# GpSimd makes every third low part of the weights in the first block of a two-block network

## The chip, the cores and the metric

One NeuronCore of a Trainium2 chip runs the kernel. The metric is the device time of one execution in microseconds, the median of several runs; less is better. The engines are named as in the profile: PE (TensorE), ACT (ScalarE), DVE (VectorE), POOL (GpSimd), SP (SyncE, which here issues DMAs).

## What is computed

Two networks follow each other on 256 tokens of width 1024, all in fp32. The first block has two layers; each multiplies the normed tokens by `w_in`, runs three kinds of attention over the parts, and multiplies the result by `w_out`:

```
def hybrid_layer(x, norm_w, w_in, ..., w_out):
    h = rmsnorm(x, norm_w)
    proj = jnp.matmul(h, w_in).astype(jnp.float32)
    (aq, ak, av, ag, bq, bk, bv, bg, cq, ck, cv, co, cg, ci, cf) = jnp.split(proj, cuts, axis=-1)
    ya = moba_attention(aq, ak, av) * silu(ag)          # 8 heads, softmax with a slope per head
    yb = head_norm(retention(rotate(bq), rotate(bk), bv), ret_norm_w) * silu(bg)
    yc = head_norm(mlstm(silu(conv(cq)), silu(conv(ck)), cv, ci, cf) * sigmoid(co), ...) * silu(cg)
    return x + jnp.matmul(concat([ya, yb, yc]), w_out)
```

The second block (two layers of gated feed-forward, attention and convolution, steered by modulation vectors `c @ w_ada`) takes the rest of the time; the change does not touch it.

## The kernel before

Tokens lie transposed in SBUF, 128 channels on the partitions. Every fp32 product is made of three matmuls in a faster format: each operand is split in a high part, rounded to that format, and a low part, the remainder; high x high, high x low and low x high are summed in PSUM (lines 412 to 414, and 443 to 445 where the weights are the moving operand).

The weights stream in from HBM, once, in the order of their use. They are cut into 628 numbered pieces of up to 1024 columns on 128 partitions. `Weights.load` (line 278) has SP load a chunk into one of five buffers `wraw`. `Weights.ahead` splits a piece into two tiles of a pool with four buffers: ACT copies it into `whi` (line 296), DVE subtracts `whi` from it into `wlo` (line 297). `get` calls `ahead` for two pieces beyond the one that is wanted, so the splits of piece i are put into the program ahead of the matmuls of piece i - 2. Each engine works through its instructions in the order of the program; waits on semaphores hold them back. The pieces called ada (16 of the first 104) are not split: DVE multiplies and sums them directly (line 558).

The first block uses pieces 0 to 103: 0 to 52 in layer 0, 53 to 103 in layer 1. `dense` and `dense_tok` run the products; after each step of the contraction they call `side.hook`, which puts a small step of the attention work into the program (generators `mlstm`, `retention`, `moba_items`, `heads_b`, `heads_c`). So DVE's queue holds, in one order: splits, ada pieces, evacuation of products (rotation at lines 838 to 845, of which `bkp` is one result), and attention steps (`put` of scores at line 826, row maxima at line 877, head norms at lines 704 to 718, and line 855).

GpSimd has little to do in the first block: after three memsets it issues the DMAs of 24 decay and slope tables, one for each head (`table`, line 638, three buffers; for the first four also a copy of one column at line 637 that orders the DMA). A table is asked for in the program where its use stands, and its DMA waits for the reader of the table three before it (line 826 or 877, on DVE). Elsewhere, in the second block's attention, GpSimd runs casts and subtractions of 128 columns (lines 1232 to 1234).

Of the kernel before, what the change touches and what calls it, by code (L numbers as in the profile page):

```python
# [9 lines left out]
F32 = mybir.dt.float32  # L10
F32R = mybir.dt.float32r
AF = mybir.ActivationFunctionType
OP = mybir.AluOpType
# [142 lines left out]
def piece_floats(s):  # L156
    return len(s[3]) * sum(n for _, n in s[4])
# [73 lines left out]
def tile_hybrid_then_dit(ctx: ExitStack, tc: tile.TileContext, wst, xT, ctxT, c_d, cols_d, base_d, first_d, heads_d,  # L231
                         mix_d, rpb_d, out, dbg=None):
    nc = tc.nc
    PE, ACT, DVE, POOL, SP = nc.tensor, nc.scalar, nc.vector, nc.gpsimd, nc.sync
# [22 lines left out]
    class Weights:  # L257
# [24 lines left out]
        def ahead(self, upto):  # L282
            while self.split < min(upto, len(self.pieces)):
                i = self.split
                c, at, s = self.pieces[i]
                while self.loaded <= c:
                    self.load()
                f = piece_floats(s)
                r = self.raw[c]
                if s[0] in "at":  # L290
                    self.parts[i] = r
                else:
                    pool, nm = (self.late, "late") if (self.keys[i][0][0], self.keys[i][1][:3]) in LATE else (wsp, "w")
                    hi = pool.tile([128, PIECE], F32R, name=nm + "hi")
                    lo = pool.tile([128, PIECE], F32R, name=nm + "lo")
                    ACT.activation(hi[:, :f], r[:, at:at + f], AF.Copy)  # L296
                    DVE.tensor_tensor(lo[:, :f], r[:, at:at + f], hi[:, :f].bitcast(F32), op=OP.subtract)  # L297
                    k = len(s[3])
                    self.parts[i] = tuple(x[:, :f].rearrange("p (k c) -> p k c", k=k) for x in (hi, lo))
                self.split += 1  # L300
                if i + 1 == len(self.pieces) or self.pieces[i + 1][0] != c:
                    while self.loaded < min(c + RAW_BUFS, len(chunks)):
                        self.load()
# [1271 lines left out]
```

## Time and profile before

| | |
|---|---|
| median of 3 runs | 2225.05 us (2223.63 to 2230.49) |
| the profiled execution | 2223.87 us, span 2222.1 us |
| busy share of the span | PE 99%, DVE 72%, ACT 42%, POOL 6% |
| granted TensorE clock, mean | 0.998 |
| line 297 on DVE, `wlo` | 460 instructions, 539.5 us |
| first block | about 0 to 325 us of the span |

All times below are of the profiled execution, in us from the start of the span. A row of the timeline gives the start, the duration, the engine, the line, the operation and what it writes and reads with its size; in brackets stands how long the engine was idle before it, and what ended that. Matmuls are pipelined, so PE counts as busy also where it runs below its pace. An instruction that is held inside the engine, for a port for instance, has a longer duration; it does not show as idle time.

### The profile page before, as it was taken

The page shows a single profiled execution, that of the slowest core. Times are in us where ns is not written, and L with a number is a line of the kernel's source. Part 1 is how long each engine was busy: PE and PEld are TensorE (multiplying, and loading weights), DVE is VectorE, ACT ScalarE, POOL GpSimd, SP SyncE. Part 2 cuts the span into 40 slices and gives each one's busy share as a digit, 9 for nine tenths or more (in the row PEclk, how much of TensorE's full clock was granted, in tenths as well). Part 3 has the DMA queues.
Part 4 walks back from the last instruction along what each step waited for, and adds up shares of the span by engine and source line. Part 5 has one row for each costly group of instructions (what it writes and reads, how often), then busy time and mean ns, then how long its engine had stood idle before and what let it go on. Part 6 is the DMA issues. An engine that isn't in the chain of part 4 may idle for free.

```text
span 2222.1 us, 33972 instructions
## 1 busy us (share of the span) xinstructions
PE 2192.7 (99%) x13010; PEld 1915.7 (86%) x13010; DVE 1610.6 (72%) x2922; ACT 943.1 (42%) x1546; POOL 131.0 (6%) x283
## 2 busy tenths in 40 slices
PE   8999999999999999999999999999999999999998
PEld 7898898888889877788988888988888898899998
DVE  7998989758848966547773766776577588767555
ACT  7465464212333366524432223332222344755444
POOL 1000000000000144100000000000000012300000
PEclk9999999999999999999999999999999999999999
DMA  8565557546642221234353556254456433255563
GB/s 271 180 203 182 184 173 228 174 137 214 205 140 72 95 72 51 68 102 161 103 177 116 183 180 188 87 180 154 134 187 191 140 110 114 65 182 179 190 198 114
DMA packets 99282, 337.99 MB, mean 152 GB/s; under 512 B 11312, under 2 KB 15664, under 8 KB 99120
## 3 DMA queue, kind: packets, MB, share of 16 engines
q1 hardware_dynamic: 95600, 326.39, 45.5%
q0 software_dynamic: 2976, 8.92, 1.3%
q8 instruction: 102, 1.67, 0.3%
q14 instruction: 60, 0.49, 0.1%
q10 hardware_dynamic: 544, 0.52, 0.1%
HBM read 334.74 MB, written 1.05 MB: 151 GB/s over the span
## 4 chain that ended last, share of the span: by engine, by line
PE 84%; issue 7%; DVE 6%; ACT 1%; DMA 1%; POOL 0%; DVEq 0%; SPq 0%; ACTq 0%; POOLq 0%
PE psd L413 22%; PE psd L412 22%; PE psd L414 22%; PE psd L396 3%; PE psd L397 3%; PE psd L395 3%; PE pso L1282 2%; DVE wlo L297 2%; PE pst L1270 1%; PE psd L443 1%; PE psd L444 1%; PE psd L445 1%; PE pss L1236 1%; DMA table<-in_heads_dram 1%; PE pss L1237 1%
## 5 line engine op out<-in xcount | busy, mean ns | idle before, releaser
L412 PE MATMUL psd<-hh,whi 128*128 128x512 f32 (+1 forms) x2240 | 770.2, 344 | 0.3 <-DVE XT L1031 0.2
L413 PE MATMUL psd<-hl,whi 128*128 128x512 f32 (+1 forms) x2240 | 768.3, 343 | 0.0
L414 PE MATMUL psd<-hh,wlo 128*128 128x512 f32 (+1 forms) x2240 | 766.7, 343 | 0.6 <-DVE wlo L297 0.5
L297 DVE TENSOR_TENSOR wlo<-wraw,whi 128x1024 fp32r<-128x1024 f32 (+2 forms) x460 | 539.5, 1176 | 231.8 <-ACT whi L296 228.1
L296 ACT ACTIVATE whi<-wraw 128x1024 fp32r<-128x1024 f32 (+2 forms) x460 | 468.1, 1020 | 553.1 <-PE psd L413 375.8
L414 PEld LDWEIGHTS psd<-hh,wlo 128*128 128x128 f32 x2240 | 420.3, 188 | 52.9 <-DVE wlo L297 1.0
L412 PEld LDWEIGHTS psd<-hh,whi 128*128 128x128 f32 x2240 | 420.5, 188 | 52.3 <-issue 1.2
L413 PEld LDWEIGHTS psd<-hl,whi 128*128 128x128 f32 x2240 | 420.7, 188 | 51.6 <-issue 1.0
L558 DVE CUSTOM_DVE_ANT_0 prod<-wraw,rows,cols 128x1024 f32<-128x1024 f32 x256 | 328.5, 1283 | 122.1 <-DMA wraw<-in_wst_dram 115.8
L412 PE MATMUL psd<-ah,whi 128*128 128x512 f32 (+1 forms) x576 | 207.8, 361 | 0.0
L413 PE MATMUL psd<-al,whi 128*128 128x512 f32 (+1 forms) x576 | 207.8, 361 | 0.0
L414 PE MATMUL psd<-ah,wlo 128*128 128x512 f32 (+1 forms) x576 | 207.8, 361 | 0.0
L1107 ACT ACTIVATE silu<-psd 128x512 f32<-128x512 f32 (+1 forms) x88 | 47.9, 544 | 228.1 <-PE psd L414 221.6
L413 PEld LDWEIGHTS psd<-al,whi 128*128 128x128 f32 x576 | 108.1, 188 | 16.9
L414 PEld LDWEIGHTS psd<-ah,wlo 128*128 128x128 f32 x576 | 108.1, 188 | 16.9
L412 PEld LDWEIGHTS psd<-ah,whi 128*128 128x128 f32 x576 | 108.1, 188 | 16.7
L585 DVE SCALAR_TENSOR_TENSOR XT<-psd,mods,XT 128x256 f32<-128x256 f32 x216 | 93.3, 478 | 39.9 <-PE psd L414 25.4
L371 ACT ACTIVATE ah<-silu 128x512 fp32r<-128x512 f32 (+1 forms) x88 | 50.4, 574 | 158.3 <-DVE silu L1108 157.9
L443 PE MATMUL psd<-whi,hh 128*128 128x512 f32 (+1 forms) x224 | 88.1, 394 | 10.4 <-ACT whi L296 7.7
L1108 DVE TENSOR_TENSOR silu<-psd,silu 128x512 f32<-128x512 f32 (+1 forms) x88 | 54.7, 622 | 57.3 <-ACT silu L1107 57.3
L444 PE MATMUL psd<-whi,hl 128*128 128x512 f32 (+1 forms) x224 | 87.0, 388 | 0.0
L445 PE MATMUL psd<-wlo,hh 128*128 128x512 f32 (+1 forms) x224 | 85.4, 386 | 0.0
(341 smaller groups left out, 2985.2 us busy)
## 6 DMA issues: line engine op xcount, KB each, us to landing
wraw<-in_wst_dram SPq DMA_DIRECT2D x564, 512.0 KB, 4.0
wraw<-in_wst_dram SPq DMA_DIRECT2D x48, 384.0 KB, 3.1
table<-in_heads_dram POOLq DMA_DIRECT2D x24, 192.0 KB, 3.3
rows<-in_cvec_dram SPq DMA_DIRECT2D x6, 512.0 KB, 5.7
rpb<-in_rpb_dram POOLq DMA_DIRECT2D x24, 128.0 KB, 2.4
wraw<-in_wst_dram SPq DMA_DIRECT2D x8, 264.0 KB, 4.2
wraw<-in_wst_dram SPq DMA_DIRECT2D x8, 256.0 KB, 2.7
XT<-in_xT_dram SPq DMA_DIRECT2D x4, 256.0 KB, 5.3
```

The lines of the kernel that those rows point to most:

```text
L296: ACT.activation(hi[:, :f], r[:, at:at + f], AF.Copy)
L297: DVE.tensor_tensor(lo[:, :f], r[:, at:at + f], hi[:, :f].bitcast(F32), op=OP.subtract)
L395: PE.matmul(p[:, n0:n1], hi, rh[:, k, n0:n1], start=k == 0, stop=False)
L396: PE.matmul(p[:, n0:n1], hi, rl[:, k, n0:n1], start=False, stop=False)
L412: PE.matmul(o, hi[:, kk, c], rh[kr][:, n0:n1], start=first and k == 0, stop=False)
L413: PE.matmul(o, hi[:, kk, c], rl[kr][:, n0:n1], start=False, stop=False)
L414: PE.matmul(o, lo[:, kk, c], rh[kr][:, n0:n1], start=False, stop=last and k == total - 1)
L443: PE.matmul(p, lh[:, k, c], hi[:, kk], start=k == 0, stop=False)
L444: PE.matmul(p, ll[:, k, c], hi[:, kk], start=False, stop=False)
L445: PE.matmul(p, lh[:, k, c], lo[:, kk], start=False, stop=k == 7)
L558: DVE.tensor_tensor_reduce(v(prod()), v(r), rows[s], 1.0, col("b_ada_2", b), op0=OP.mult, op1=OP.add, accum_out=mods.rearrange("p l c s -> ...
L585: DVE.scalar_tensor_tensor(XT[:, d, c], p[:, c], mods[:, l, 8 * m + d, h:h + 1], XT[:, d, c], op0=OP.mult, op1=OP.add)
```

## The change

In `Weights.ahead` the engine of the subtraction depends on the piece. In the first block (the key of the piece is `("first", layer)`), pieces whose number leaves 2 when divided by 3, from number 11 on, are subtracted by GpSimd; all others stay with DVE. The high parts stay with ACT.

```
                     ACT.activation(hi[:, :f], r[:, at:at + f], AF.Copy)
-                    DVE.tensor_tensor(lo[:, :f], r[:, at:at + f], hi[:, :f].bitcast(F32), op=OP.subtract)
+
+                    eng = POOL if self.keys[i][0][0] == "first" and i % 3 == 2 and i > 8 else DVE
+                    eng.tensor_tensor(lo[:, :f], r[:, at:at + f], hi[:, :f].bitcast(F32), op=OP.subtract)
```

## Rows read from the trace of the kernel before

**Rows 1.** Busy time by stretch: span, PE, PEld, DVE, ACT, POOL, clock, DMA share, GB/s.
```profile
0.00:325.00 325.00, 309.85 (x2174) 285.47 (x2175) 286.04 (x611) 198.59 (x347) 19.32 (x35) 1.00 0.62 202
235.00:245.00 10.00, 7.67 (x58) 7.07 (x57) 9.31 (x24) 1.44 (x2) 1.08 (x2) 1.00 0.29 93
```

**Rows 2.** Groups of instructions, 0 to 325 us: busy us, mean ns, idle before.
```profile
L297 DVE TENSOR_TENSOR wlo<-wraw,whi 128x1024 fp32r<-128x1024 f32 (+1 forms) x92 | 107.0, 1172 | 8.2 <-ACT whi L296 7.9
```

**Rows 3.** Timeline, 78 to 85 us, piece 29: start us, duration us, engine, line.
```profile
78.45 1.06 ACT L296 ACTIVATE whi<-wraw 128x1024 fp32r<-128x1024 f32 x1 [1.15 <-PE psd L413]
78.88 2.36 DVE L297 TENSOR_TENSOR wlo<-wraw,whi 128x1024 fp32r<-128x1024 f32 x2
...
81.15 0.69 DVE L855 SCALAR_TENSOR_TENSOR yc<-gC,yc 128x512 f32<-128x512 f32 x1
...
84.43 0.48 PE L774 MATMUL pss<-bqr,bkp 128*128 128x256 f32 x1 [0.62 <-DVE bkp L845]
```

**Rows 4.** Timeline, 232 to 251 us, pieces 83 and 86.
```profile
232.84 1.23 DVE L297 TENSOR_TENSOR wlo<-wraw,whi 128x1024 fp32r<-128x1024 f32 x1 [1.35 <-ACT whi L296]
...
233.98 1.28 DVE L558 CUSTOM_DVE_ANT_1 prod<-wraw,XT,cols 128x1024 f32<-128x1024 f32 x1
...
236.34 1.06 ACT L296 ACTIVATE whi<-wraw 128x1024 fp32r<-128x1024 f32 x1 [2.01 <-DMA wraw<-in_wst_dram]
237.39 0.87 DVE L845 TENSOR_TENSOR bkp<-t,t 64x256 f32<-64x256 f32 x2
...
237.86 0.70 PE L774 MATMUL pss<-bqr,bkp 128*128 128x256 f32 x2 [1.76 <-DVE bkp L845]
...
249.38 1.22 DVE L297 TENSOR_TENSOR wlo<-wraw,whi 128x1024 fp32r<-128x1024 f32 x1
250.51 0.68 DVE L704 TENSOR_REDUCE mu<-yc 128x8 f32<-128x512 f32 x1
```

**Rows 5.** GpSimd's nearest operations: a line (min/median/max ns), and one row of the timeline.
```profile
L1234 POOL TENSOR_TENSOR qpad<-y,qpad x72: 445/458/1506, 761.7 to 1920.6; 64x128 fp32r<-64x128 f32 x72
...
88.78 0.18 POOL L637 COPY table<-mcol 128x1 f32<-128x1 f32 x1 [47.38 <-DVE t L826]
```

**Rows 6.** Timeline, 41 to 47 us, piece 14: high part, first use of its low part.
```profile
41.48 1.04 ACT L296 ACTIVATE whi<-wraw 128x1024 fp32r<-128x1024 f32 x1
...
46.72 0.40 PE L445 MATMUL psd<-wlo,hh 128*128 128x512 f32 x1
```

**Rows 7.** Timeline of the second block, around 790 and 901 us, GpSimd and DVE.
```profile
790.36 0.45 POOL L1234 TENSOR_TENSOR qpad<-y,qpad 64x128 fp32r<-64x128 f32 x1
790.44 1.46 DVE L297 TENSOR_TENSOR wlo<-wraw,whi 128x1024 fp32r<-128x1024 f32 x1
...
901.08 1.22 DVE L297 TENSOR_TENSOR wlo<-wraw,whi 128x1024 fp32r<-128x1024 f32 x1
901.10 1.51 POOL L1234 TENSOR_TENSOR qpad<-y,qpad 64x128 fp32r<-64x128 f32 x1
902.21 0.42 DVE L1242 TENSOR_TENSOR m<-m,nsink 128x1 f32<-128x1 f32 x1
```

**Rows 8.** Timeline, 46 to 50 us, piece 17.
```profile
46.27 1.06 ACT L296 ACTIVATE whi<-wraw 128x1024 fp32r<-128x1024 f32 x1
46.76 0.87 DVE L769 SCALAR_TENSOR_TENSOR ckp<-t,t 64x256 f32<-64x256 f32 x2
...
47.97 1.22 DVE L297 TENSOR_TENSOR wlo<-wraw,whi 128x1024 fp32r<-128x1024 f32 x1
...
49.11 0.48 DVE L761 SCALAR_TENSOR_TENSOR t<-cpad,cols,t 128x256 f32<-128x256 f32 x1
```

**Rows 9.** Tables: landing times of line 638; timeline of piece 95 and of a table's use.
```profile
DMA to landing us min/median/max: 2.6/3.3/5.9
...
273.26 1.06 ACT L296 ACTIVATE whi<-wraw 128x1024 fp32r<-128x1024 f32 x1 [1.33 <-DMA wraw<-in_wst_dram]
278.99 0.28 DVE L877 CUSTOM_DVE_ANT_0 t<-pss,table 128x128 f32<-128x128 f32 x1
```

## The prediction

> **What bounds the kernel now.** I read the busy time by stretch first, to see which engine has no room where the change acts. The first block is the first 325 us of the span; VectorE (DVE) is busy for 286.0 of them and TensorE (PE) for 309.9 [rows 1]. Both look full, so the second look is at a short stretch of it: from 235 to 245 us PE is busy 7.67 of 10 us while DVE has 9.31 [rows 1]. The reader is to see that there PE waits for DVE, not DVE for PE. The grouped instructions of the same 325 us say what DVE does: the subtraction of line 297 that makes the low parts is its largest item, 92 instructions and 107.0 us [rows 2]. Last comes the timeline, instruction by instruction, around the places where PE stands idle with DVE as releaser: 0.62 us ahead of 84.43 [rows 3], 1.76 us ahead of 237.86 [rows 4]. After 325 us no moved piece is left, and nothing of the rest changes but its starting time.
>
> **What is moved.** Pieces with number i, i % 3 == 2, i > 8, that belong to the first block and aren't ada pieces: 26 of them, 10 in layer 0 (11, 14, 17, 20, 29, 32, 38, 41, 47, 50) and 16 in layer 1 (from 53 to 101), 24 with 1024 columns and 2 with 528. No arithmetic is added or left out.
>
> **What leaves DVE.** One such subtraction holds DVE from 249.38 to the next start at 250.51 [rows 4], 1.13 us; in proportion 0.58 us for 528 columns. 24 x 1.13 + 2 x 0.58 = 28.3 us leave DVE's queue. That is the most the change can give, and only where DVE has work ready behind.
>
> **What GpSimd needs.** Nothing of this size runs on GpSimd (POOL) in the trace. The nearest row is its two-input operation on 128 columns, median 458 ns; a one-column copy takes 0.18 us [rows 5]. As a fixed part and a slope, (458 - 180) / 127 = 2.19 ns a column, so 180 + 1023 x 2.19 = 2.42 us for 1024 columns and 1.33 for 528 (estimates). From below I bound it by DVE's own 1.22 us [rows 4], from above by eight times the 458 ns row, 3.66 us. I take 2.42, since fixed part and slope both come from rows.
>
> The Trainium skill ("GPSIMD Engine Reference", Performance versus the Vector engine) gives 4497 ns for a two-input add of 2048 elements; half of it, 2.25 us, is an estimate from that page, and the sum below would be some 2 us smaller by it.
>
> **Does the low part come late for PE?** For all 26 pieces I set the end of the high part (ACT, line 296), plus a wait for the running DVE instruction, plus GpSimd's time, against PE's first matmul on that low part. Piece 14 is the tightest: its high part ends at 42.52, GpSimd would end near 45.0, PE needs it at 46.72 [rows 6]: 1.7 us to spare. The others have 2.7 to 12. So a slower low part costs nothing by itself; what hides it is the lead of two to three pieces with which the splits run ahead. Even the 3.66 us price would leave 0.5 us at this piece.
>
> **What it costs DVE.** The trace shows that the two engines exclude each other when both read two operands from SBUF. At 790.36 a GpSimd operation of two inputs is running; the subtraction of 1024 columns that DVE starts at 790.44 takes 1.46 us, not 1.22. At 901.10 it is the other way round: DVE's subtraction has begun 0.02 us earlier, and GpSimd's operation takes 1.51 us, to 0.3 us behind DVE's end; DVE's next two-input instruction, on a single column, takes 0.42 us and ends with GpSimd's [rows 7]. So each waits for the other's whole stream, and GpSimd gets in at the next boundary. I take the slope's part, 2.24 us, as the time for which it keeps DVE's two-input instructions out (those with an operand in PSUM go on, and so do all of one input).
>
> The Trainium skill ("SBUF — State Buffer", Who interferes with whom) has this as a lock for the whole instruction. In the first of these rows DVE is free some 0.14 us ahead of GpSimd's end, a little less than the page has; by the page the sum would grow by about 2 us.
>
> Now I walk the 26 places in the timeline: a hold of 2.24 us from the end of the high part (or of the DVE instruction then running), and by how much DVE's next two-input instruction starts later than it did. Three of them:
> - Piece 17 [rows 8]: the high part ends at 47.33, DVE's line 769 at 47.63; GpSimd holds to 49.87. Line 297 stood at 47.97; without it line 761 could start 1.1 us ahead of its 49.11, but it is held to 49.87: 0.76 us later than before, with the subtraction gone.
> - Piece 29 [rows 3]: the high part ends at 79.51, DVE is in piece 28 until 80.1, GpSimd holds to 82.3. Line 855 started at 81.15: 1.2 later. Behind it comes bkp, for which PE stood idle at 84.43.
> - Pieces 83 and 86 [rows 4]: 83 holds from 232.86 to 235.10, line 558 started at 233.98: 1.12 later. Piece 86 has its high part at 237.40, in the middle of DVE's rotation; line 845, which writes the bkp that PE waits for at 237.86, would stand behind it for up to 2.2 us, of which 1.13 come back only at 249.38.
>
> Over the 26 the delay of that instruction is 31.0 us in sum. At 11 pieces the removed subtraction lay ahead of it, and the delay is net; at the other 15 it came later, out of a backlog, and is given back then: 14 x 1.13 + 0.58 = 16.4 us. Net, DVE is 14.6 us later, not 28 earlier.
>
> How much of that sets the end? DVE idles 39 of the 325 us [rows 1], and a delay ahead of an idle stretch is lost in it. I count the pieces behind which PE is seen to wait for DVE: 17 (0.8), 29 (1.2), 50 and 53 (1.2 + 0.6), 68 (0.9), 83 and 86 (1.1 + 1.1), 89, 92 and 95 (0.1 - 0.6 + 1.2): 7.6 us. The other 7.0 go into idle time or into the lead of the weights; if that cover is gone, they are paid too.
>
> **The tables behind it on GpSimd's queue.** GpSimd issues the 24 DMAs of line 638; until now it ran ahead of the program, held by the three buffers alone. Now each issue stands behind the low parts that the program has put before it, and those wait for ACT. A table lands 3.3 us after its issue in the median, 5.9 at most [rows 9]. The high part of piece 95 ends at 274.32, and GpSimd is done with it at 277 to 278.5; the table used at 278.99 [rows 9] is issued behind it and lands near 281 to 282, some 2 to 3 us late. One more, behind piece 89, is about 2 us late; the other 22 are in time by the same walk, or late by 1.5 us at most. DVE stands for these in a stretch where PE waits for it, but part of the wait replaces the delay above: I count 1.5 of the 5 us, with 0 and 10 as ends.
>
> **Sum.** The profiled execution took 2223.87 us, 2222.1 of them its span, and is 1.2 below the median of 2225.05. 7.6 + 1.5 = 9.1; 2223.9 + 9.1 = 2233.0; against the median, 2234.
>
> **Rivals.**
> - DVE is relieved (faster): the hold costs it little, since it works from PSUM or waits meanwhile, and the subtractions are gone. For it: DVE is full, and at 15 pieces time comes back. Worth 1.13 us a piece where PE waits behind DVE, nine and a half of the pieces listed: 11 us, 2214. Against it: the rows of exclusion. It decides if GpSimd's hold is under the 1.13 us saved, or if DVE's next instructions read PSUM.
> - It cancels: DVE's 14.6 us fall into its idle time and the weights' lead of 2 to 12 us, the tables land in time: 2222 to 2228.
> - GpSimd at its upper price: 1.24 us more hold a piece, 26 x 1.24 = 32 us on DVE, half of it on the path (as 7.6 of 14.6): 16 more, 2250. Every table behind a low part is then late as well.
>
> **How the numbers follow.** Forecast 0.43, cancels 0.30, relief 0.17, upper price 0.10. A measurement here tells some 0.3%, 6.7 us, from no change; 0.07 of the forecast's chance lies within that. So faster 0.17, same 0.37, slower 0.46. With GpSimd's lower price (1.22 us, hold near 1) the walk gives DVE back some 20 us, half of it on the path: 2215; with the upper, 2250. The range 2213 to 2252 takes in both and leaves out the tails of relief and of the upper price.
>
> **What would show it.** GpSimd's rows of line 297 near 2.4 us each, longer by what they wait for DVE. DVE's two-input lines in the first block (297, 558, 761, 855, 845) longer by 1 to 2 us at some places, and its busy time in the 325 us not 28 us lower but about as high, since a held instruction counts as busy. PE's stall ahead of line 774 near 238 us longer, not shorter. Tables waiting behind line 297 on GpSimd, and DVE's line 877 with a wait for the DMA. Stretches after the first block as they were, only later. The forecast would be wrong if GpSimd's and DVE's line 297 overlap at full speed, or if the first block ends earlier with DVE's lines unchanged in length.

## The result, and the profile after

| | before | changed |
|---|---|---|
| median of 3 runs | 2225.05 us | 2253.2 us (2251.79 to 2262.52) |
| ratio to before | | 1.0138 [1.0119, 1.0157] |
| the profiled execution | 2223.87 us, span 2222.1 us | 2251.79 us, span 2250.0 us |
| first block's end: start of the last matmul on piece 108's low part (the fifth piece behind the block) | 334.07 us | 361.97 us |

The changed kernel is slower by 1.4%, 28 us. All of it arises in the first block: the last matmul on the low part of piece 108 starts 27.9 us later than before, and matmuls at 500, 1000 and 1700 us are late by 27.9 to 28.1 us.

Busy time by stretch, changed kernel (stretch, span, PE, PEld, DVE, ACT, POOL, granted clock, DMA share, GB/s):
```profile
0.00:325.00 325.00, 288.09 (x1944) 264.00 (x1944) 277.56 (x546) 181.68 (x317) 83.84 (x60) 0.97 0.57 191
...
56.00:68.00 12.00, 5.66 (x31) 5.29 (x29) 10.10 (x17) 6.76 (x12) 2.34 (x1) 0.73 0.53 175
...
255.00:267.00 12.00, 6.21 (x32) 5.64 (x31) 11.64 (x24) 1.06 (x1) 1.19 (x3) 0.72 0.40 135
```
The same 325 us hold less of the program than in [rows 1]. Up to the first block's end, which is the same work but for the 26 subtractions, the kernel before and then the changed one have:
```profile
0.00:334.07 334.07, 318.92 (x2250) 294.54 (x2250) 294.04 (x631) 202.23 (x355) 19.32 (x35) 1.00 0.61 199
0.00:361.97 361.97, 324.91 (x2249) 299.89 (x2250) 305.97 (x609) 203.07 (x357) 86.24 (x61) 0.97 0.56 186
```
DVE is busy for 11.9 us more although 28 us of its work are gone. PE stands idle for 37.1 us instead of 15.1; summed over its waits, 29.3 of them are for DVE, where it was 7.2. The granted clock was 1.00 throughout; now it averages 0.97, and it is lowest around two long stalls of PE (0.73 and 0.72).

Groups of instructions, changed kernel, 0 to 325 us (count, busy us, mean ns, idle before):
```profile
L299 DVE TENSOR_TENSOR wlo<-wraw,whi 128x1024 fp32r<-128x1024 f32 (+1 forms) x60 | 76.0, 1269 | 8.5 <-ACT whi L296 8.3
```
and GpSimd's new line by its forms (count, ns min/median/max, first and last start):
```profile
L299 POOL TENSOR_TENSOR wlo<-wraw,whi x26: 1310/2440/4088, 30.1 to 325.9; 128x1024 fp32r<-128x1024 f32 x24, 128x528 fp32r<-128x528 f32 x2
```
(Line numbers behind 296 are 2 higher than before.) GpSimd's median of 2.44 us is the 2.42 that was forecast; its maximum of 4.09 is a wait for DVE. DVE's remaining subtractions take 1269 ns in the mean where they took 1172 [rows 2].

Timeline, changed kernel (start us, duration us, engine, line; in brackets the idle time before it and what ended that):
```profile
49.74 3.24 POOL L299 TENSOR_TENSOR wlo<-wraw,whi 128x1024 fp32r<-128x1024 f32 x1 [3.29 <-ACT whi L296]
...
50.63 2.64 DVE L763 SCALAR_TENSOR_TENSOR t<-cpad,cols,t 128x256 f32<-128x256 f32 x1
...
59.40 2.34 POOL L299 TENSOR_TENSOR wlo<-wraw,whi 128x1024 fp32r<-128x1024 f32 x1 [6.42 <-ACT whi L296]
59.55 3.28 DVE L560 CUSTOM_DVE_ANT_1 prod<-wraw,XT,cols 128x1024 f32<-128x1024 f32 x1 [1.17 <-DMA wraw<-in_wst_dram]
...
62.76 0.41 DVE L801 TENSOR_TENSOR t<-pso,T 128x256 f32<-128x256 f32 x1
63.09 0.28 DVE L802 TENSOR_TENSOR t<-pso,T 128x128 f32<-128x128 f32 x1
...
63.51 0.66 PE L798 MATMUL pso<-base,mcol 128*128 128x128 f32 x2 [6.34 <-DVE t L802]
...
239.69 2.40 POOL L299 TENSOR_TENSOR wlo<-wraw,whi 128x1024 fp32r<-128x1024 f32 x1 [7.21 <-ACT dn L812]
239.70 2.41 DVE L813 TENSOR_TENSOR dn<-dn,mcol 128x4 f32<-128x4 f32 x1
...
261.63 1.22 PE L776 MATMUL pss<-bqr,bkp 128*128 128x256 f32 x2 [5.79 <-DVE bkp L847]
```
The reader is to see two things. First, DVE's two-input instructions last until GpSimd's operation beside them is done: 2.64 us for 256 columns, and 2.41 for an instruction of four columns. Second, at 59.55 line 560 stands ahead of 801 and 802, for which PE waits: besides its wait of 1.17 us for the weights and its hold of 2 us, it is in front of them in DVE's queue. The order of the instructions isn't that of the kernel before: the framework orders them when it builds the program, and with 26 instructions on another engine it chose another order in the first block, on DVE, PE and ACT. PE's stall of 1.76 us [rows 4] is 5.79 us here.

### The profile page after: what moved, and what is told of

Its sections match the earlier page's. It is cut to its first block, busy times and chain, and to the rows that moved or that the text cites. A ratio compares the mean times of both kernels' runs of the same rounds, so it can differ in the third digit from the quotient of the medians.

```text
span 2250.0 us, 33999 instructions
## 1 busy us (share of the span) xinstructions
PE 2198.4 (98%) x13010; PEld 1921.2 (85%) x13010; DVE 1620.5 (72%) x2896; ACT 942.4 (42%) x1546; POOL 198.2 (9%) x309
## 3 DMA queue, kind: packets, MB, share of 16 engines
HBM read 334.74 MB, written 1.05 MB: 149 GB/s over the span
## 4 chain that ended last, share of the span: by engine, by line
PE 88%; DVE 8%; issue 1%; ACT 1%; DMA 1%; DVEq 0%; POOL 0%; SPq 0%; ACTq 0%; POOLq 0%
PE psd L414 23%; PE psd L415 23%; PE psd L416 23%; PE psd L397 3%; PE psd L399 3%; PE psd L398 3%; DVE wlo L299 2%; PE pso L1284 2%; PE psd L445 1%; PE psd L447 1%; PE psd L446 1%; PE pst L1272 1%; DVE prod L560 1%; DMA wraw<-in_wst_dram 1%; PE pss L1238 1%
## 5 line engine op out<-in xcount | busy, mean ns | idle before, releaser
L299 DVE TENSOR_TENSOR wlo<-wraw,whi 128x1024 fp32r<-128x1024 f32 (+2 forms) x434 | 515.6, 1191 | 232.8 <-ACT whi L296 229.1
```

The lines of the kernel that those rows point to most:

```text
L299: eng.tensor_tensor(lo[:, :f], r[:, at:at + f], hi[:, :f].bitcast(F32), op=OP.subtract)
```

## The experiments

Theory L: GpSimd's operation and DVE shut each other out, and that makes the loss. Rival O: the new order makes it. Rival T: the tables behind it on GpSimd's queue. "Held" below sums over the first block by how much DVE's instructions are longer than the same instructions, one by one, in a kernel of the same order that moves nothing (the kernel before, or ord_after_dve), where it is over 0.1 us; the changed kernel has 36.8 us at 21. "End" is how much later than 334.07 us the last matmul on piece 108's low part starts. Both come from one execution each, the ratio from all.

| kernel | ratio to before, 95% | end, us | held, us (instructions) |
|---|---|---|---|
| ord_before | 1.0116 [1.0099, 1.0133] | +20.5 | 36.2 (22) |
| ord_after_dve | 1.0071 [1.0055, 1.0086] | +12.9 | none moved |
| ord_after_memset | 0.9992 [0.9982, 1.0001] | -5.0 | 0.8 (1) |
| held_memset | 0.9972 [0.9961, 0.9982] | -6.2 | 2.1 (3) |
| held_copy | 0.9989 [0.9974, 1.0003] | -2.9 | 12.9 (19) |
| held_quarters | 1.0037 [1.0026, 1.0049] | +6.7 | 22.4 (47) |
| held_eighths | 1.0096 [1.0078, 1.0115] | +21.5 | 14.4 (65) |
| held_twice | 1.0306 [1.0279, 1.0333] | +72.6 | 78.4 (46) |
| changed_again | 1.0144 [1.0122, 1.0167] | +30.0 | 35.9 (21) |
| order_again | 1.0108 [1.0090, 1.0126] | +22.0 | 35.4 (23) |
| only_others | 1.0064 [1.0045, 1.0083] | +10.2 | 19.9 (14) |
| only_listed | 1.0057 [1.0037, 1.0077] | +13.0 | 15.8 (9) |

**The order held as before.** An engine's instructions are chained in a given order; the chain only orders their issue.
```
+    ins = [traced[k] for k in at if str(traced[k].engine) == "EngineType." + e]
+    for a, b in zip(ins, ins[1:]):
+        tc.add_manual_dep(b, a.name, mybir.DependencyInfo(mybir.DependencyClass.NoSync, mybir.DependencyReason.DATA), reason="pin")
```


> The changed kernel (the 26 low parts on GpSimd), but with the instructions of VectorE, ScalarE, TensorE and SyncE held in the order that they have in the kernel before. Theory L (lock: what GpSimd's operation takes from VectorE's two-input instructions makes the whole loss): the order doesn't matter, so about 2250, the 2253 of the changed kernel. Theory O (the order that the framework gives the instructions anew makes most of it): only my forecast's own terms are left, 2226 to 2236, and the granted clock stays at 1.0 in the first block. If it comes below 2222, the moved work is a gain that the new order spoils.

Measured: 2248.61 us (before beside it 2224.8), the end of the first block 20.5 us late. So with the order of before most of the loss is still there; theory O falls as the main cause, and my own 2226 to 2236 with it. The profile shows where DVE stands. Timeline, ord_before:
```profile
28.93 2.61 POOL L299 TENSOR_TENSOR wlo<-wraw,whi 128x1024 fp32r<-128x1024 f32 x1 [24.61 <-ACT whi L296]
...
29.05 2.64 DVE L761 TENSOR_SCALAR t<-cpad,cols 128x256 f32<-128x256 f32 x1
...
58.86 2.35 POOL L299 TENSOR_TENSOR wlo<-wraw,whi 128x1024 fp32r<-128x1024 f32 x1 [6.20 <-ACT whi L296]
59.02 0.42 DVE L801 TENSOR_TENSOR t<-pso,T 128x256 f32<-128x256 f32 x1
59.36 0.28 DVE L802 TENSOR_TENSOR t<-pso,T 128x128 f32<-128x128 f32 x1
...
61.03 1.28 DVE L560 CUSTOM_DVE_ANT_1 prod<-wraw,XT,cols 128x1024 f32<-128x1024 f32 x1
...
195.13 4.41 POOL L299 TENSOR_TENSOR wlo<-wraw,whi 128x1024 fp32r<-128x1024 f32 x1 [4.50 <-ACT whi L296]
195.27 0.47 DVE L763 SCALAR_TENSOR_TENSOR t<-cpad,cols,t 128x256 f32<-128x256 f32 x1
...
195.66 1.21 DVE L299 TENSOR_TENSOR wlo<-wraw,whi 128x1024 fp32r<-128x1024 f32 x1
...
196.80 0.47 DVE L763 SCALAR_TENSOR_TENSOR t<-cpad,cols,t 128x256 f32<-128x256 f32 x1
...
197.75 2.07 DVE L767 SCALAR_TENSOR_TENSOR cqs<-t,t 128x256 f32<-128x256 f32 x1 [0.39 <-ACT t L765]
```
At 29.05 an instruction with one SBUF tensor as its input takes 2.64 us; the same one took 0.38 in the kernel before:
```profile
30.07 0.38 DVE L759 TENSOR_SCALAR t<-cpad,cols 128x256 f32<-128x256 f32 x1
```
At 59.02 and 59.36 instructions with an operand in PSUM run beside GpSimd at their usual length. At 195.13 it is the other way round: three DVE instructions follow each other without a gap, GpSimd gets in between none of them, and takes 4.41 us. That isn't the rule. In most places GpSimd gets in as soon as DVE's running instruction ends, and the next one is held, though it too follows without a gap; ord_before:
```profile
290.55 3.42 POOL L299 TENSOR_TENSOR wlo<-wraw,whi 128x1024 fp32r<-128x1024 f32 x1 [7.65 <-ACT whi L296]
...
291.65 3.40 DVE L299 TENSOR_TENSOR wlo<-wraw,whi 128x1024 fp32r<-128x1024 f32 x1
```
What decides between the two stays open.

**The order of the changed kernel, all low parts on DVE.** The same chain, with the other order, in the kernel before; the 26 subtractions aren't part of that order and stand on DVE where the framework puts them.

> The kernel before (all low parts on VectorE), with the instructions of VectorE, ScalarE, TensorE and SyncE held in the order that they have in the changed kernel; the 26 subtractions stand on VectorE where the framework puts them among these. No GpSimd operation, so no lock. Theory L: no loss from the order, 2223 to 2230. Theory O: the late places of the order remain (TensorE waiting about 6 us for line 802 near 57 us and for line 847 near 256 us) and with them 15 to 28 us: 2240 to 2253.

Measured: 2239.06 us, 1.0071, 9 us above theory L's range and 1 below theory O's. The order, with the places of the 26 in it, costs 14 us while DVE has all its work.

**The order of the changed kernel, GpSimd reads nothing.**
```
-                    eng.tensor_tensor(lo[:, :f], r[:, at:at + f], hi[:, :f].bitcast(F32), op=OP.subtract)
+                    if eng is POOL:
+                        POOL.memset(lo[:, :f].bitcast(F32), 0.0)
```


> The changed kernel with the order of all its instructions held as it is, but the 26 subtractions on GpSimd replaced by a memset of the same tile, which reads nothing (about 0.95 us by the memsets of 1024 columns at the start of the trace); so the low parts of these 26 pieces are left out of the result. Theory L: with nothing read from SBUF the lock is gone, and VectorE has 28 us less to do: 2215 to 2228. Theory O: the order is still that of the changed kernel, so at least half of the loss stays: 2238 to 2250.

Measured: 2221.62 us, 0.9992. The order of the changed kernel costs little (2.4 us against the next kernel) when DVE is rid of 28 us of work and isn't held.

**The order of before, with a memset.** The same edit, every engine, GpSimd too, in the order of ord_before.

> The order of every engine, GpSimd included, as in ord_before (that is, the order of the kernel before), with the 26 subtractions on GpSimd replaced by a memset of the same tile, which reads nothing; the low parts of these 26 pieces are left out of the result. It differs from ord_before in nothing but what GpSimd reads and how long it takes. Theory L (lock): the whole 24 us of ord_before go, and what is left is the relief of VectorE: 2214 to 2225 (2214 if the rival 'VectorE is relieved' priced it rightly, near 2222 if TensorE has no use for the time). Theory T (tables, or GpSimd's queue): GpSimd's instructions stand where they stood, so 5 us or more of the loss stay: 2230 or above.

Measured: 2219.26 us, 0.9972 and significantly below before. Nothing of the 24 us is left. What PE waited for in the first 355 us (total us, times, longest), held_memset:
```profile
PE psd L448 <- ACT whi L296: 7.5, 1, 7.5
PE pst L690 <- DVE yc L723: 1.0, 1, 1.0
PE pst L895 <- DVE sums L904: 0.7, 1, 0.7
PE pso L801 <- DVE t L805: 0.4, 1, 0.4
...
```
and ord_before:
```profile
PE psd L445 <- ACT whi L296: 7.4, 1, 7.4
PE pso L798 <- DVE t L802: 4.5, 2, 2.6
PE pss L776 <- DVE bkp L847: 4.0, 2, 2.3
PE psd L416 <- DVE wlo L299: 2.6, 3, 1.2
PE psd L447 <- DVE wlo L299: 2.3, 2, 1.5
PE psd L415 <- DVE hl L374: 1.7, 1, 1.7
...
```
The first wait, 7.5 us, is the kernel's start. Behind it PE waits for DVE in many small places, and 4.9 us of it are for low parts that DVE itself still makes. DVE waits for tables 2.1 us in held_memset and 3.6 in ord_before, and 1.8 in the kernel before: rival T is worth 1.5 to 1.8 us there. In the changed kernel it is worth nothing: 1.2 us.

DVE is hardly held by the memsets, and where it is, by instructions of one tensor alone: all three are TENSOR_SCALAR. The longest, held_memset:
```profile
38.00 1.13 DVE L755 TENSOR_SCALAR mcol<-mcol 128x8 f32<-128x8 f32 x1 [0.29 <-ACT mcol L754]
...
38.13 0.97 POOL L300 MEMSET wlo<- 128x1024 f32 x1
```
A memset also waits for no operand and is done early, so the memset alone doesn't rule out that late low parts, or buffers `wraw` that come free late, make the loss. The waits speak against it: PE waits for no low part that GpSimd makes, neither in ord_before nor in the changed kernel, and ACT and DVE wait for raw weights 13.2 us in ord_before and 4.3 in the changed kernel, against 11.6 in the kernel before.

**GpSimd reads one operand.**
```
-                        POOL.memset(lo[:, :f].bitcast(F32), 0.0)
+                        POOL.tensor_copy(lo[:, :f], r[:, at:at + f])
```


> As ord_before, but GpSimd copies the raw weights into the low part's tile: one operand is read instead of two, and no high part is subtracted for these 26 pieces. If only an instruction of two inputs keeps VectorE out: as held_memset, 2214 to 2225. If any instruction of GpSimd that reads and writes SBUF does: by its duration, 2235 to 2250, and VectorE's instructions beside it are 1 to 2 us long again.

Measured: 2222.45 us. DVE is held by the copy too, at 19 places, but for 0.3 to 1.1 us each, 12.9 us in all, since the copy takes 1.05 us in the median, less than half of the subtraction's 2.44. The time falls in the first branch, but not for its reason. It is 3 us above the memset's, which is nearly as long (0.95 us): what GpSimd reads counts, and for how long.

**The subtraction in quarters, and in eighths.**
```
+                    step = f // 4 if eng is POOL else f
+                    for q in range(0, f, step):
+                        ins = eng.tensor_tensor(lo[:, q:q + step], r[:, at + q:at + q + step], hi[:, q:q + step].bitcast(F32), op=OP.subtract)
```


> As ord_before, with each of the 26 subtractions on GpSimd cut into four of a quarter of the columns (256, or 132). Theory L with release at each instruction's end: one of VectorE's instructions is held for 0.6 us at most, where it was held for 2.2; if VectorE has work from SBUF ready each time it meets all four, and the sum is about the same: 2243 to 2250; if it comes through between them with work that hurries, 2228 to 2240. If the hold doesn't end with the instruction, no change against ord_before.

Measured: 2232.95 us, 1.0037; in the middle of the second branch.

> As held_quarters, with eighths of the columns (128, or 66). Against held_memset (no lock), the lock cost 29 us in one piece of work and 14 us in quarters. If what counts is the longest time for which one VectorE instruction is held (0.28 us here): 6 to 8 us above held_memset, 2225 to 2228, no difference to the kernel before. If it is GpSimd's whole time in the lock, which the eighths don't shorten: 2232 or above, as the quarters.

Measured: 2249.82 us, 1.0096. That is the second branch by its bound, but 17 us above the quarters that it named, so its reason doesn't hold either. DVE's instructions are held less than in quarters (14.4 us, none for more than 0.34), yet the block ends 21.5 us late. GpSimd's groups (count, busy us, mean ns) are the nearest to a reason; held_quarters:
```profile
L301 POOL TENSOR_TENSOR wlo<-wraw,whi 128x256 fp32r<-128x256 f32 x96 | 96.1, 1031 | 140.3 <-ACT whi L296 120.4 <-DVE t L810 13.8 <-ACT y L699 6.1
```
and held_eighths:
```profile
L301 POOL TENSOR_TENSOR wlo<-wraw,whi 128x128 fp32r<-128x128 f32 x192 | 123.7, 680 | 130.3 <-ACT whi L296 130.3
```
A piece takes GpSimd 4 x 1.03 = 4.1 us in quarters and 8 x 0.68 = 5.4 in eighths, where it took 2.7 in one instruction: the median quarter takes 0.74 us and the median eighth 0.47, but at each GpSimd may wait for DVE anew, 5.7 and 5.5 us at the longest. Waits of the loads on SP's queue, held_eighths:
```profile
SPq L278 <- POOL wlo L301: 114.6, 25, 8.2
```
and ord_before:
```profile
SPq L278 <- POOL wlo L299: 78.0, 22, 7.6
```
The raw weights' buffer comes free only when its low part is made, so the next load is later. It shows: ACT and DVE wait for raw weights 23.9 us in held_eighths, where it was 13.2. The larger part of these waits, held_eighths and then ord_before:
```profile
ACT whi L296 <- DMA wraw<-in_wst_dram: 18.7, 11, 3.4
...
ACT whi L296 <- DMA wraw<-in_wst_dram: 11.9, 6, 4.8
```
DVE also waits for tables 5.2 us instead of 3.6. That this makes the eighths' loss is argued from these rows; no run separates it.

**The subtraction twice.**
```
+                    for again in range(2 if eng is POOL else 1):
+                        ins = eng.tensor_tensor(lo[:, :f], r[:, at:at + f], hi[:, :f].bitcast(F32), op=OP.subtract)
```


> As ord_before, with each of the 26 subtractions on GpSimd issued twice (the second one writes the same again). Theory L: a second hold of 2.24 us for each piece, 26 x 2.24 = 58 us on VectorE without any work taken off it; with the share on the path that ord_before shows (24 us lost beside 35 us of hold and 28 us taken away), 2280 to 2305. My rival 'GpSimd at its upper price' had half of the added hold on the path: 2278. If only the lateness of the low parts counted, 2250 to 2258, since their lead is 2 us and more.

Measured: 2294.73 us, within theory L's range and 46.1 us above ord_before. The reason given for the range holds only in part: DVE's instructions are held 78.4 us in all, 42.2 more than in ord_before and not 58, so more is lost than is held. Here late weights add to it: PE waits 1.3 us for low parts that GpSimd makes, and ACT 22.2 us for raw weights instead of 11.9. Busy time over the first 355 us, held_twice:
```profile
0.00:355.00 355.00, 295.32 (x1885) 267.00 (x1886) 306.01 (x526) 176.07 (x303) 154.19 (x85) 0.94 0.52 172
```
The granted clock, 1.00 in the kernel before, is 0.94 here: with more and longer stalls of PE it falls more often.

**What the new order adds.** The changed kernel and ord_before once more, beside each other.

> The changed kernel as it is, beside the next run on the same chip, to size the part of the new order. Lock alone (theory L): the same as order_again, within 0.15%. Lock, and an order that makes it dearer: 4 to 8 us above order_again, since the first block of the changed kernel ends 27.9 us later than before and that of ord_before 20.5 us.

> The kernel of ord_before once more (the 26 low parts on GpSimd, every other engine in the order of the kernel before): 2244 to 2250 by the first measurement.

Measured: 2258.9 and 2251.79 us, 7.1 us apart; the first block's ends are 30.0 and 22.0 us late, as 27.9 and 20.5 in the first pair. The intervals of the two ratios touch (1.0122 to 1.0167, 1.0090 to 1.0126), so the 7 us rest on two pairs that agree more than on either interval. 2251.79 is 2 us above what I expected; the kernel before took 2229.65 beside it, 5 us more than beside the first measurement.

**The two halves of the pieces.** The condition of line 298 with a list of pieces, the order as before.
```
-                    eng = POOL if self.keys[i][0][0] == "first" and i % 3 == 2 and i > 8 else DVE
+                    eng = POOL if self.keys[i][0][0] == "first" and i % 3 == 2 and i in (17, 29, 50, 53, 68, 83, 86, 89, 92, 95) else DVE
```


> As ord_before (the other engines in the order of the kernel before), but only the 16 pieces go to GpSimd behind which my walk saw no wait of TensorE for VectorE, and for which it counted nothing (11, 14, 20, 32, 38, 41, 47, 56, 59, 62, 65, 74, 77, 80, 98, 101). If the prediction's step 'the other 7 us go into idle time or into the lead of the weights' holds: no loss, 2222 to 2229 (or some 3 us of gain). If any hold of VectorE in this block sets TensorE back, seen before or not: 16 of 26 parts of 20 to 24 us, 12 to 15 us, 2237 to 2243.

> The other half: only the 10 pieces go to GpSimd that the prediction counted (17, 29, 50, 53, 68, 83, 86, 89, 92, 95). By the prediction's list they carry all of the loss, 7.6 us and 1.5 for the tables: 2232 to 2236, and the two halves add up to that. If the loss is spread evenly: 10 of 26 parts, 8 to 9 us, the same time, so that the two halves together make 20 to 24 us.

Measured: only_others 2240.03 us, 1.0064, 14 us above before where the prediction counted nothing; only_listed 2240.81 us, 1.0057. The second is 5 us above what both branches gave it. The two losses add up to 1.2%, that of ord_before; the ends (10.2 and 13.0 us) add up to 23.2 us, beside 20.5 and 22.0 in its two measurements. So the loss is spread over the pieces and not tied to the places where PE was seen to wait before; but it isn't even: by the ends a piece of the list costs 1.3 us and one of the others 0.64. Piece 11, one of the "others", shows how it goes. Timeline, only_others:
```profile
29.38 2.60 POOL L299 TENSOR_TENSOR wlo<-wraw,whi 128x1024 fp32r<-128x1024 f32 x1 [25.06 <-ACT whi L296]
...
29.49 2.64 DVE L761 TENSOR_SCALAR t<-cpad,cols 128x256 f32<-128x256 f32 x1
...
32.79 0.27 DVE L742 TENSOR_SCALAR rows<-rows 4x256 f32<-4x256 f32 x1
...
33.12 0.47 PE L747 MATMUL pso<-base,rows 4*128 4x4 f32 x5 [0.87 <-DVE rows L742]
33.38 1.21 DVE L299 TENSOR_TENSOR wlo<-wraw,whi 128x1024 fp32r<-128x1024 f32 x1
...
34.65 0.74 PE L447 MATMUL psd<-wlo,hh 128*128 128x512 f32 x2 [0.75 <-DVE wlo L299]
```
The hold at 29.49 moves all that DVE has queued behind it: the rows of line 742, for which PE then waits 0.87 us, and the low part of piece 9, which DVE makes and which PE wants at once (0.75 us).

## Why the prediction was wrong

The side was right: slower was forecast, and slower it is. The size was not: 9 us were forecast, 28 measured, and 2253.2 lies just outside the range that ended at 2252.

- **GpSimd's price.** Right: 2.42 us forecast, 2.34 to 2.49 where it isn't hindered. The rival of the upper price gave 2250, near the result, by a price that wasn't there.
- **The hold.** Near in size: 31.0 us over 26 places forecast, 36.2 at 22 instructions in ord_before and 36.8 at 21 in the changed kernel. That instructions "with an operand in PSUM go on" is what 59.02 shows. "And so do all of one input" was wrong: two of line 761 were held for 2.26 and 2.13 us.

  The Trainium skill ("SBUF — State Buffer", Who interferes with whom) lists tensor_scalar among the instructions that can take the port which GpSimd shares, and says that an instruction with two SBUF inputs meets a GpSimd instruction that reads SBUF, not one that only writes it. Both agree with the runs here: 2.64 us at 29.05, and 2.1 us held in all beside the memsets, by three TENSOR_SCALAR and no two-input instruction. I had read past the first.
- **GpSimd "gets in at the next boundary".** Right in most places, as at 291.65 of ord_before; not at 195.13, where three instructions of DVE went ahead and GpSimd took 4.41 us.
- **Netting the hold against the work removed.** This is the step that failed most: its term, the 7.6 us that I put on the path, measured 20.5 us with the order held. I set 16.4 us given back against 31.0 us of hold and took half of the rest as path. The runs give the two different shares. held_memset takes the subtractions off DVE and hardly holds it: 28.3 us removed bring the first block's end 6.2 us forward, 22%. ord_before adds the hold: from -6.2 to +20.5, 26.7 us beside 34.1 us more of hold (36.2 less 2.1), 78%. In these two runs time given to the queue was mostly lost in waits behind it, and time taken from it mostly paid. The share isn't a constant: beside held_memset the copy costs 3.3 us for 10.8 us more of hold (31%), the quarters 12.9 for 20.3 (64%), and the eighths 27.7 for 12.3, so there the hold can't be all.
- **"The other 7.0 go into idle time or into the lead of the weights".** Wrong: only_others, for which this gave nothing, is 14 us slower, 10.2 at the first block's end. I had checked the lead of the moved pieces, 1.7 to 12 us, and not that of the pieces which DVE still makes behind them.
- **The order.** I took each engine's instructions to stand in the order of the kernel before. The new order costs 7 us more beside the hold: a term that was missing. The trace of before couldn't show it; the price of an unforeseen order is 7 us here, and 14 if DVE keeps all its work.
- **The clock.** No term of mine. The granted clock of the first 355 us is 0.97 in the changed kernel, 0.99 in ord_before, 1.00 in held_memset. In the changed kernel four stretches, 20.5 us together, run at the lower of its two levels (1.2 of 2.4 GHz); each begins during a stall of PE of 2.2 to 6.3 us or within 1 us behind it. PE's waits make 22.0 of the 27.9 us, and 6.0 are longer busy time (324.9 us instead of 318.9). That is what the clock can have cost, set off by the stalls; no run separates it.
- **The tables.** Forecast were 1.5 us more of waiting. In the changed kernel DVE waits less for tables than before, 1.2 us instead of 1.8; in ord_before it is 3.6. So the term isn't there in the kernel that it was meant for.
- **The rival of relief** was sized at 11 us. Without a hold it is 6: of 2225 us PE is busy for 99%, and DVE's relief bought no more. So no split of this subtraction between the two engines was found that beats the kernel before; for these 26 pieces in this order, the 0.28% of held_memset, which doesn't compute the low parts, is what DVE's relief without a hold was worth.

With the shares measured, my own sum would be 0.78 x 31.0 - 0.22 x 28.3 + 7.1 = 25.1 us, against 28. That is no check of the shares, which come from the same runs; it says that the hold's share and the order were what was missing.

## What to carry to other kernels

When work is moved to an engine that excludes the first one, sum the holds and the relief apart: in a block where both engines feed a full TensorE, most of a hold was paid in ord_before (78%) and little of the relief came back in held_memset (22%). Ask of a held instruction not whether PE waits for it, but what stands behind it in its queue with little lead. And ask whether the instructions will stand in the same order after the change: fix the order, or count some us for it.

## What the hardware showed that I had not expected

- The exclusion works in both directions, and by what is read: a GpSimd memset of 1024 columns (0.95 us) held DVE for 2.1 us in all 26 places together, a copy (1.05 us) for 12.9, the subtraction (2.44 us) for 36.2. Once DVE's stream without gaps kept GpSimd out for 2 us, though mostly GpSimd comes in at the next boundary.
- Shorter GpSimd instructions are no cure: in quarters the loss falls from 20.5 to 6.7 us, in eighths it is 21.5 again.
- Near the end of the kernel, far from all moved work, TensorE runs about 4% slower in some executions at a granted clock of 1.00: 427 matmuls in 50 us instead of 444. The stretch from 2100 to 2150 us, ord_before:
```profile
2100.00:2150.00 50.00, 50.00 (x427) 50.00 (x426) 27.95 (x34) 20.44 (x27) 0.00 (x0) 1.00 0.59 187
```
and the changed kernel:
```profile
2100.00:2150.00 50.00, 50.00 (x444) 50.00 (x443) 28.56 (x35) 21.63 (x27) 0.00 (x0) 1.00 0.60 194
```
Four of the fourteen profiled executions show it. It adds some 5 to 8 us to such an execution, and is why the first block's end is compared beside the times. What it comes from stays open.
